# Two plain tile pairs per FFN, a weight queue that moves within a job, and a new order in the opening and the tail of a one-core decoder layer

## The chip, the core and the metric

One core of a Trainium2 chip runs the whole program. The metric is device time in microseconds (us) of one execution; a profiled execution gives the rows shown below. The engines are TensorE (PE in the rows, its weight loads PEld), VectorE (DVE), ScalarE (ACT), GpSimd (POOL, whose queue also issues some transfers) and SyncE (SP, which issues the others).

## What is computed

One decoder layer for a prompt of 1024 rows and for 8 single-row samples that share its weights, in float32:

```python
def pre(i, t):
    return rms_norm(t, norm_g[i]) * (1 + mod[:, :, 3 * i + 1]) + mod[:, :, 3 * i]   # mod = adaLN(c)
x = x + 0.5 * mod[:, :, 2] * swiglu(pre(0, x), ffn1_up, ffn1_down)
y, states = token_mix(pre(1, x), caches, ...)       # dilated attention + gMLP
x = x + mod[:, :, 5] * y
x = x + 0.5 * mod[:, :, 8] * swiglu(pre(2, x), ffn2_up, ffn2_down)
# after the layer: rms_norm(x, final_g); outputs also hold the key/value caches, one row further
def swiglu(h, w_up, w_down):
    a, b = jnp.split(h @ w_up, 2, axis=-1)
    return (jax.nn.silu(a) * b) @ w_down
```

The model width is 1024, the FFN width 2816 (22 tiles of 128), two FFNs and a token mix between them.

## The kernel before

The activations are held transposed, features on the partitions, 1032 columns (1024 prompt rows and 8 samples) as two halves of 516, each of two quarters of 258. Every float32 operand is split into a leading part (`hi`, a cast by ACT) and a remainder (`lo`, a subtraction by DVE), and each product is three matmuls: hi by hi, hi by lo, lo by hi.

**Up projection** (`Up`). For each of the 22 tiles the two blocks `a` and `b` of the weight are multiplied with the input. A *plain* tile pair goes through eight steps per half of the columns, each step 12 matmuls (four slices of the contraction by three) of 258 columns. A *factored* tile uses seven products in place of eight, each of two blocks of 12 matmuls, one per half. Its weights need sums of weight blocks (`take`, lines 701 to 705, DVE) and its activations need combinations of their quarters (`blend`, DVE and ACT). The first `PLAINS = 3` tiles are plain, in the order of `turns` (tile, half): (0,0), (1,0), (0,1), (1,1), (2,0), (2,1). Meanwhile the operands of the second half and the combinations are made by generators in `hi_q`, which `tick` moves on; there are two ticks in each block of 12 matmuls. `blend` for the second half waits with its last two operands for the end of the plain turns of each half (`plain_done`), since their buffers come from there. A tile's weight units are prepared six units ahead at most, and as buffers come free. `banks` gives the first PSUM bank of each plain turn; gates (lines 764 to 768) read a bank before the next turn may write it. After the combinations the adaLN stream of the later modulations starts in FFN 1.

**Down projection** (`Down`). The 22 tiles are five parts of 6, 4, 4, 4 and 4. Parts 1 to 4 in the order of the program (here called part 0 to part 3) run as eight whole-tile jobs each (`whole`, `mm_thirds`): 1032 columns in three pieces of 344, K slices by three pieces by three matmuls, so 54 in a job of part 0 and 36 in a job of parts 1 to 3. Line 321 is the matmul that needs the remainder of the weights. After a job DVE reads the sample columns (line 950) and adds the product to the residual in six pieces (line 954). The last part runs in narrower jobs.

The weights of the down projection come through a queue. SP loads a slab into one of two raw buffers; `advance` casts an operation's piece of it (line 249, ACT) and puts its subtraction `low_part` (line 252, DVE) on the list `late`, two ticks off; `pump` calls `advance` if the slab was issued at least two counts of `clock` ago and fewer than four operations are under way. `run` calls a job, counts the clock up, calls `pump` and gives one tick. A job that needs an operation whose subtraction is still on the list makes `get_wt` put it into the queue at once. A slab is given back, and the next load issued, when its last subtraction is queued. In part 0 an operation serves one job, in parts 1 to 3 two.

```python
if i not in raws or clock[0] - born[i] < 2 or st["op"] - st["done"] >= 4:
    return                                  # pump
...
while st["low"] <= i:                       # get_wt
    late.popleft()[1]()
```

The split of the next part's operands (`Down.split`, lines 872 and 874) is a generator of `hi_q` too; in part 0 it starts at the seventh tick.

**Opening.** Row statistics (`row_scale`: line 465 on DVE, 468 on ACT, 474 on POOL), scaling (`over_rms`) and transposes (`turned_x`) of four row tiles make the first half of the columns; the samples go through `smp`; the first four adaLN groups (`first_mods`, line 394, and `ada_fin`, lines 416 to 431) give shift and scale for `modulate` and `sample_norm`. Four steps of the first plain turn (`up1.step`) are placed by hand between them.

**Tail.** `finish_last` turns the last quarter back, scales rows by 1/rms and stores them; `scaled` (line 1887) is DVE, line 1924 ACT. Line 1876 applies `final_g` to the first 512 features of that quarter ahead of time.

Of the kernel before, what the change touches and what calls it, by code (L numbers as in the profile page):

```python
# [11 lines left out]
AF = mybir.ActivationFunctionType  # L12
# [53 lines left out]
def trunk(ctx: ExitStack, tc, a, o):  # L66
    nc = tc.nc
# [37 lines left out]
    def ends(t, n=4):  # L105

        return t.rearrange("p k (q t) -> p k q t", q=2)[:, :, :, 256:]
# [8 lines left out]
    def dealing(**kw):  # L116
        for k, v in kw.items():
            deal[k] = deque(v)
# [30 lines left out]
    clock = [0]  # L149
# [34 lines left out]
    for g in range(3):  # L184
        n = (LS[g] - 1) * 512
        for b in range(NS):
            s = a[f"cache_kv_g{g}"][0, b, 1:].rearrange("r k h d -> (r k h d)")
            t = o[6 + g][0, b, :LS[g] - 1].rearrange("r k h d -> (r k h d)")
# [3 lines left out]
            t = t.rearrange("(r c) -> r c", r=rows)  # L192
# [71 lines left out]
    def pump():  # L264
        if st["op"] >= st["last"]:
            return
        i, s = ops[st["op"]]
        if i not in raws or clock[0] - born[i] < 2 or st["op"] - st["done"] >= 4:
            return
        advance()  # L270
# [39 lines left out]
    def mm_thirds(w, j, K, act):  # L310

        ps = bank("three")[:, :, :CW]
        wt = get_wt(w)
        for k in range(K):
            wh, wl = wt.at(k, j)
            h, l = act(k)
            for c in range(3):
                cs = slice(c * CW, (c + 1) * CW)
                mm_f(ps[:, c], wh, h[:, cs], start=(k == 0), stop=False)  # L319
                mm_f(ps[:, c], wh, l[:, cs], start=False, stop=False)  # L320
                mm_f(ps[:, c], wl, h[:, cs], start=False, stop=(k == K - 1))  # L321
            if k < K - 1:
                tick()
                if k % 2:
                    tick()
        return ps
# [334 lines left out]
    class Up:  # L661

        ACC = (0, 1, 0, 2, 0, 2, 1)
        AHEAD = 6
        PLAINS = 3

        STEPS = ((0, 0, 0), (1, 0, 1), (0, None, 2), (1, None, 3), (2, 1, 0), (3, 1, 1), (2, 6, 2), (3, 6, 3))

        def __init__(self, w, dst):
            self.w = w[0].rearrange("(k p) c -> p k c", p=128)  # L670
            self.dst = dst
            self.turns = [(n, (p,)) for n, p in ((0, 0), (1, 0), (0, 1), (1, 1), (2, 0), (2, 1))]
            self.turns += [(n, (0, 1)) for n in range(self.PLAINS, NF)]
            self.units = [(n, j) for n in range(NF) for j in range(4 if n < self.PLAINS else 7)]
            self.base = {n: self.units.index((n, 0)) for n in range(NF)}
            self.left = [4 if n < self.PLAINS else 1 for n, j in self.units]
            self.n, self.next, self.top, self.gone = len(self.units), 0, 0, [0, 0]
            self.raw, self.wt, self.tmp = {}, {}, {}
# [302 lines left out]
    up1, down1 = Up(a["ffn1_up"], g_d), Down(a["ffn1_down"], g_d, xs_d, 16, XS)  # L981
# [26 lines left out]
    up2, down2 = Up(a["ffn2_up"], g_d), Down(a["ffn2_down"], g_d, x2_d, 64, None)  # L1008
# [45 lines left out]
    def turned_x(t, h, qs, ks=range(4)):  # L1054

        for k in ks:
            f = h * 4 + k
            nc.tensor.transpose(qs[k][:, t % 4 * 128:(t % 4 + 1) * 128], XN[t // 2][:, t % 2, f * 128:(f + 1) * 128], ident)
# [19 lines left out]
    def sample_norm(h):  # L1078
        v = SXT[0][:, 4 * h:4 * h + 4]
        nc.vector.tensor_tensor(v, v, MOD[:, 8 + 4 * h:12 + 4 * h, 1:9], op=ALU.mult)  # L1080
        for p in range(2):
            c = 4 * p
            nc.vector.tensor_tensor(ends(XT[p][h]), v[:, :, c:c + 4].rearrange("p k (q t) -> p k q t", q=2),
                                    MOD[:, 4 * h:4 * h + 4, 1 + c:5 + c].rearrange("p k (q t) -> p k q t", q=2), op=ALU.add)
# [9 lines left out]
    def steps(g, n=99):  # L1094
        for _ in range(n):
            if next(g, 0) == 0:
                return
# [3 lines left out]
    fins = {g: ada_fin(g) for g in range(4)}  # L1101
    XT[0], XT[1] = ([four(qb(name="x")) for h in range(2)] for p in range(2))
    smp = sample_rows()
# [7 lines left out]
    steps(mods[2])  # L1111
    steps(fins[2], 1)
    row_scale(1)
    steps(smp)
    got = [bank("nx") for k in range(4)]
    over_rms(0, 0)
    turned_x(0, 0, got)
    steps(fins[2])
    row_scale(2)
    over_rms(1, 0)  # L1120
    turned_x(1, 0, got)
    sample_norm(0)
    row_scale(3)
    for t in (2, 3):
# [13 lines left out]
    up1.step(0, 0, 0)  # L1138
    up1.prepare(2)
    up1.step(0, 1, 0)  # L1140
    steps(mods[3])
    got = [PSB[:, i, :] for i in (4, 6, 5, 7)]
    for t in range(4):
        turned_x(t, 1, got, (0,))
    steps(fins[1])
    steps(fins[3], 1)
    for t in range(4):
        turned_x(t, 1, got, (1,))
    up1.step(0, 2, 0)
    up1.prepare(3)  # L1150
    steps(fins[3])
    up1.step(0, 3, 0)
    sample_norm(1)
    for t in range(4):
        turned_x(t, 1, got, (2, 3))
    for k in range(4):
        modulate(0, 4 + k, got[k])
    steps(halves(0, 1, 1, 2))
    dealing(nx=(4, 5, 6, 7))

    def second_half():
        yield
# [36 lines left out]
        if n >= 8 and j == 2:  # L1199
            pump_copy()  # L1200

    up1.run(hook1, (2, 2, 4, 2, 6, 4), 4)

    def last1(m, p, qs):
        stat_pair(XT[p][m // 4][:, m % 4], m, p)
# [648 lines left out]
    fgc = R0[:, :8]  # L1854
# [6 lines left out]
        if n >= 4 and j == 2:  # L1861
            pump_copy()

    up2.run(hook2, (2, 4, 6, 2, 6, 4))

    SPOT = {(0, 0): (1024, 1540), (1, 0): (1540, 1798), (1, 1): (1024, 1282)}

    def last2(m, p, qs):
        key = p, qs[0]
        last = key == (1, 1)  # L1870
        c0, c1 = qs[0] * QW, (qs[-1] + 1) * QW
        x = XT[p][m // 4][:, m % 4, c0:c1]
        stat_add(x, m, key, ph[:, slice(*SPOT[key])], last and m == 7)
        if last and m < 4:
            v = x[:, :256]
            nc.scalar.activation(v, v, AF.Copy, scale=fgc[:, m:m + 1])
        if m == 7:
            hi_q.append(finish_last() if last else finish(p, qs))

# [5 lines left out]
    def scaled(row, w, hf, q, r):  # L1885
        f4 = lambda v: v.rearrange("p (f c) -> p f c", f=4)
        nc.vector.scalar_tensor_tensor(f4(row[:w, hf * 512:(hf + 1) * 512]), f4(q[:w, :]), r,
                                       f4(fgb[:w, hf * 512:(hf + 1) * 512]), op0=ALU.mult, op1=ALU.mult)
# [21 lines left out]
    def finish_last():  # L1910

        blks = [v for v in BLOCKS if v[0] // QW == 1]
        banks = {(n, hf): PSB[:, n * 2 + hf, :] for n in range(3) for hf in range(2)}
        for n, (b, w) in enumerate(blks[:2]):
            turned(1, b, w, 0, banks[n, 0])
        rs = yield from rstd((1, 1), shifted(blks, 1), 0, 0)
        for n, (b, w) in enumerate(blks[:2]):
            turned(1, b, w, 1, banks[n, 1])
        b2, w2 = blks[2]
        for hf in range(2):  # L1920
            turned(1, b2, w2, hf, banks[2, hf])
        rows_ = [rows2(qb(name="y"))[:, 0, :1024] for _ in blks]
        for n, (b, w) in enumerate(blks[:2]):
            nc.scalar.activation(rows_[n][:, :512], banks[n, 0], AF.Copy, scale=rs[n])
            scaled(rows_[n], w, 1, banks[n, 1], rs[n])
            nc.sync.dma_start(out_rows(1, b, w), rows_[n])
        for hf in range(2):
            scaled(rows_[2], w2, hf, banks[2, hf], rs[2])
        nc.sync.dma_start(out_rows(1, b2, w2), rows_[2][:w2])

    down2.run(last2, [(0, (0, 1)), (1, (0,)), (1, (1,))])
# [31 lines left out]
```

## Time and profile before

| | |
|---|---|
| median of 3 runs | 2442.7 us (2440.42 to 2444.96) |
| profiled execution | 2440.93 us |
| its span, first to last instruction | 2438.9 us |
| mean granted clock of TensorE | 0.986 of full speed |

A row of the timeline begins with the start in us from the begin of the span and the duration in us, then engine, line, operation, result and operands, and in brackets how long that engine was idle before and what ended the wait. A wait row names who waited for whom, the total in us, the number of waits and the longest. A window row gives a stretch, the busy us (and number) of engines in it, then the granted clock, the busy share of the DMA engines and GB/s. The ends of matmuls are modelled and neighbouring matmuls overlap, so rates are taken from start to start.

### The profile page before, as it was taken

The numbers are of one execution on the slowest core, as the hardware profiler recorded it, in microseconds if no ns is written. First come the engines' busy times: TensorE is split into PE (matmuls) and PEld (weight loads), VectorE is DVE, ScalarE is ACT, GpSimd is POOL, SyncE is SP. The second block draws the span as 40 slices with busy tenths as digits, with TensorE's granted clock in tenths as the row PEclk, the third lists the DMA queues.
The fourth block names the chain that finished last, engine by engine and source line by source line (L and its number), as shares of the span: only waits on it lengthen the run. The fifth ranks groups of instructions, "written<-read, shape, count | busy, mean of one in ns | idle before, by whom it ended". The sixth has DMA issues, their size and how long they took to land.

```text
span 2438.9 us, 42426 instructions
## 1 busy us (share of the span) xinstructions
PE 2363.5 (97%) x18047; PEld 2272.3 (93%) x18047; DVE 1278.2 (52%) x2674; ACT 759.6 (31%) x1455; POOL 251.6 (10%) x378
## 2 busy tenths in 40 slices
PE   7999999998899999999999999999999999988999
PEld 5999999997899999999998999999999999987998
DVE  5555555563466544333252534536566666644665
ACT  4433333341111344444421131224333333411112
POOL 1200000020000200001110012221000000100003
PEclk8999999999999999999999999999999999999999
DMA  8554565454310221123221127534455552443201
GB/s 290 106 181 153 172 190 182 157 212 152 122 70 29 88 78 46 62 77 107 86 76 57 40 84 227 175 106 126 152 194 185 183 183 79 137 159 122 70 18 70
DMA packets 203670, 305.00 MB, mean 125 GB/s; under 512 B 9081, under 2 KB 146017, under 8 KB 199898
## 3 DMA queue, kind: packets, MB, share of 16 engines
q1 hardware_dynamic: 177840, 206.38, 25.8%
q0 software_dynamic: 25488, 95.83, 12.1%
q8 instruction: 141, 2.31, 0.4%
q14 instruction: 47, 0.39, 0.1%
q10 hardware_dynamic: 154, 0.09, 0.0%
HBM read 245.72 MB, written 100.53 MB: 142 GB/s over the span
## 4 chain that ended last, share of the span: by engine, by line
PE 56%; issue 3%; DVE 3%; DMA 1%; ACT 1%; POOL 1%; DVEq 0%; POOLq 0%; ACTq 0%
PE PSB L287 6%; PE PSB L740 6%; PE PSB L741 6%; PE PSB L742 6%; PE PSB L288 5%; PE PSB L289 5%; PE PSB L303 3%; PE PSB L304 3%; PE PSB L305 3%; PE PSB L321 3%; PE PSB L320 3%; PE PSB L319 3%; PE PSB L1342 1%; PE PSB L1394 1%; PE PSB L1377 1%
## 5 line engine op out<-in xcount | busy, mean ns | idle before, releaser
L740 PE MATMUL PSB<-h,lo 128*128 128x258 f32 x1264 | 361.2, 286 | 2.8 <-DVE t L765 1.5
L287 PE MATMUL PSB<-n,hi 128*128 128x258 f32 (+1 forms) x1152 | 361.7, 314 | 1.8 <-DVE s L930 1.8
L741 PE MATMUL PSB<-h,lo 128*128 128x258 f32 x1264 | 358.1, 283 | 0.3 <-DVE h L573 0.3
L742 PE MATMUL PSB<-h,lo 128*128 128x258 f32 x1264 | 357.2, 283 | 0.0
L740 PE MATMUL PSB<-h,hi 128*128 128x258 f32 x1248 | 355.9, 285 | 1.2 <-DVE t L768 1.2
L741 PE MATMUL PSB<-h,hi 128*128 128x258 f32 x1248 | 353.2, 283 | 0.0
L742 PE MATMUL PSB<-h,hi 128*128 128x258 f32 x1248 | 352.2, 282 | 0.0
L288 PE MATMUL PSB<-n,hi 128*128 128x258 f32 (+1 forms) x1152 | 349.1, 303 | 0.5 <-DVE n L546 0.5
L289 PE MATMUL PSB<-n,lo 128*128 128x258 f32 (+1 forms) x1152 | 347.4, 302 | 0.0
L321 PE MATMUL PSB<-g,lo 128*128 128x344 f32 x864 | 285.6, 331 | 41.0 <-DVE lo L252 41.0
L319 PE MATMUL PSB<-g,hi 128*128 128x344 f32 x864 | 283.8, 328 | 2.2 <-DVE t L804 1.9
L320 PE MATMUL PSB<-g,hi 128*128 128x344 f32 x864 | 284.1, 329 | 0.0
L740 PEld LDWEIGHTS PSB<-h,lo 128*128 128x128 f32 x1264 | 239.9, 190 | 16.6 <-issue 10.1
L740 PEld LDWEIGHTS PSB<-h,hi 128*128 128x128 f32 x1248 | 236.4, 189 | 13.2 <-issue 10.6
L741 PEld LDWEIGHTS PSB<-h,lo 128*128 128x128 f32 x1264 | 240.0, 190 | 0.5 <-DVE h L573 0.5
L742 PEld LDWEIGHTS PSB<-h,lo 128*128 128x128 f32 x1264 | 239.5, 189 | 0.0
L287 PEld LDWEIGHTS PSB<-n,hi 128*128 128x128 f32 x1152 | 218.2, 189 | 22.5 <-issue 17.0
L741 PEld LDWEIGHTS PSB<-h,hi 128*128 128x128 f32 x1248 | 236.7, 190 | 0.0
L742 PEld LDWEIGHTS PSB<-h,hi 128*128 128x128 f32 x1248 | 236.0, 189 | 0.0
L249 ACT ACTIVATE hi<-raw 128x1024 fp32r<-128x1024 f32 (+1 forms) x114 | 114.0, 1006 | 358.2 <-PE PSB L320 212.8
L288 PEld LDWEIGHTS PSB<-n,hi 128*128 128x128 f32 x1152 | 218.4, 190 | 1.9 <-DVE n L546 1.7
L289 PEld LDWEIGHTS PSB<-n,lo 128*128 128x128 f32 x1152 | 218.4, 190 | 0.0
(299 smaller groups left out, 4426.9 us busy)
## 6 DMA issues: line engine op xcount, KB each, us to landing
raw<-in_ffn_up_dram SPq DMA_DIRECT2D x88, 512.0 KB, 5.6
ada<-in_ada_w_dram SPq DMA_DIRECT2D x36, 1024.0 KB, 6.0
out_dram<-in_cache_kv_g_dram SPq DMA_DIRECT2D x16, 2047.0 KB, 10.9
g<-g_d POOLq DMA_DIRECT2D x22, 1032.0 KB, 5.8
g_d<-t POOLq DMA_DIRECT2D x76, 258.0 KB, 2.7
raw<-in_ffn_down_dram SPq DMA_DIRECT2D x16, 1024.0 KB, 5.0
raw<-in_w_in_dram SPq DMA_DIRECT2D x12, 1024.0 KB, 5.2
raw<-in_w_in_dram SPq DMA_DIRECT2D x18, 512.0 KB, 3.7
```

Source lines behind the costliest of these rows:

```text
L249: nc.scalar.activation(h3, v, AF.Copy)
L287: mm_f(ps, wh, ah, start=(k == 0), stop=False)
L288: mm_f(ps, wh, al, start=False, stop=False)
L289: mm_f(ps, wl, ah, start=False, stop=(k == K - 1))
L303: mm_f(ps[:, q, :], wh, h, start=(k == 0), stop=False)
L304: mm_f(ps[:, q, :], wh, l, start=False, stop=False)
L319: mm_f(ps[:, c], wh, h[:, cs], start=(k == 0), stop=False)
L320: mm_f(ps[:, c], wh, l[:, cs], start=False, stop=False)
L321: mm_f(ps[:, c], wl, h[:, cs], start=False, stop=(k == K - 1))
L740: mm_f(out, wh, ah, start=(kk == 0 and start), stop=False, **go)
L741: mm_f(out, wh, al, start=False, stop=False, **go)
L742: mm_f(out, wl, ah, start=False, stop=(kk == 3 and stop), **go)
```

## The change

`PLAINS` goes from 3 to 2: the third tile becomes a factored one in both FFNs, the turns (2,0) and (2,1) go, and the bank lists of both up projections get four entries. In `mm_thirds` the clock counts up and `pump` is called once more, after the middle slice of the contraction. In the opening the statistics, scaling and transposes of the second row tile come ahead of the third adaLN group's end and of the samples; the ends of the second and fourth group and all transposes for two feature tiles come ahead of the third hand-placed step. In the tail the samples' rows of the last block are scaled by `final_g` early, together with the prompt rows, and their first half is scaled by ACT in place of DVE.

```diff
--- before.py
+++ after.py
@@ -319,6 +319,9 @@
                 mm_f(ps[:, c], wh, h[:, cs], start=(k == 0), stop=False)
                 mm_f(ps[:, c], wh, l[:, cs], start=False, stop=False)
                 mm_f(ps[:, c], wl, h[:, cs], start=False, stop=(k == K - 1))
+            if k == K // 2 - 1:
+                clock[0] += 1
+                pump()
             if k < K - 1:
                 tick()
                 if k % 2:
@@ -662,14 +665,14 @@
 
         ACC = (0, 1, 0, 2, 0, 2, 1)
         AHEAD = 6
-        PLAINS = 3
+        PLAINS = 2
 
         STEPS = ((0, 0, 0), (1, 0, 1), (0, None, 2), (1, None, 3), (2, 1, 0), (3, 1, 1), (2, 6, 2), (3, 6, 3))
 
         def __init__(self, w, dst):
             self.w = w[0].rearrange("(k p) c -> p k c", p=128)
             self.dst = dst
-            self.turns = [(n, (p,)) for n, p in ((0, 0), (1, 0), (0, 1), (1, 1), (2, 0), (2, 1))]
+            self.turns = [(n, (p,)) for n, p in ((0, 0), (1, 0), (0, 1), (1, 1))]
             self.turns += [(n, (0, 1)) for n in range(self.PLAINS, NF)]
             self.units = [(n, j) for n in range(NF) for j in range(4 if n < self.PLAINS else 7)]
             self.base = {n: self.units.index((n, 0)) for n in range(NF)}
@@ -1111,14 +1114,14 @@
     steps(mods[2])
     steps(fins[2], 1)
     row_scale(1)
-    steps(smp)
     got = [bank("nx") for k in range(4)]
     over_rms(0, 0)
     turned_x(0, 0, got)
-    steps(fins[2])
     row_scale(2)
     over_rms(1, 0)
     turned_x(1, 0, got)
+    steps(fins[2])
+    steps(smp)
     sample_norm(0)
     row_scale(3)
     for t in (2, 3):
@@ -1138,25 +1141,23 @@
     up1.step(0, 0, 0)
     up1.prepare(2)
     up1.step(0, 1, 0)
+    steps(fins[1])
     steps(mods[3])
+    steps(fins[3], 1)
     got = [PSB[:, i, :] for i in (4, 6, 5, 7)]
     for t in range(4):
-        turned_x(t, 1, got, (0,))
-    steps(fins[1])
-    steps(fins[3], 1)
-    for t in range(4):
-        turned_x(t, 1, got, (1,))
+        turned_x(t, 1, got, (0, 1))
+    steps(fins[3])
+    sample_norm(1)
     up1.step(0, 2, 0)
     up1.prepare(3)
-    steps(fins[3])
-    up1.step(0, 3, 0)
-    sample_norm(1)
     for t in range(4):
         turned_x(t, 1, got, (2, 3))
+    up1.step(0, 3, 0)
     for k in range(4):
         modulate(0, 4 + k, got[k])
     steps(halves(0, 1, 1, 2))
-    dealing(nx=(4, 5, 6, 7))
+    dealing(nx=(4, 5, 6, 7), tr=(6, 7))
 
     def second_half():
         yield
@@ -1199,7 +1200,7 @@
         if n >= 8 and j == 2:
             pump_copy()
 
-    up1.run(hook1, (2, 2, 4, 2, 6, 4), 4)
+    up1.run(hook1, (2, 2, 4, 6), 4)
 
     def last1(m, p, qs):
         stat_pair(XT[p][m // 4][:, m % 4], m, p)
@@ -1861,7 +1862,7 @@
         if n >= 4 and j == 2:
             pump_copy()
 
-    up2.run(hook2, (2, 4, 6, 2, 6, 4))
+    up2.run(hook2, (2, 4, 6, 4))
 
     SPOT = {(0, 0): (1024, 1540), (1, 0): (1540, 1798), (1, 1): (1024, 1282)}
 
@@ -1872,8 +1873,7 @@
         x = XT[p][m // 4][:, m % 4, c0:c1]
         stat_add(x, m, key, ph[:, slice(*SPOT[key])], last and m == 7)
         if last and m < 4:
-            v = x[:, :256]
-            nc.scalar.activation(v, v, AF.Copy, scale=fgc[:, m:m + 1])
+            nc.scalar.activation(x, x, AF.Copy, scale=fgc[:, m:m + 1])
         if m == 7:
             hi_q.append(finish_last() if last else finish(p, qs))
 
@@ -1924,8 +1924,8 @@
             nc.scalar.activation(rows_[n][:, :512], banks[n, 0], AF.Copy, scale=rs[n])
             scaled(rows_[n], w, 1, banks[n, 1], rs[n])
             nc.sync.dma_start(out_rows(1, b, w), rows_[n])
-        for hf in range(2):
-            scaled(rows_[2], w2, hf, banks[2, hf], rs[2])
+        nc.scalar.activation(rows_[2][:w2, :512], banks[2, 0][:w2], AF.Copy, scale=rs[2])
+        scaled(rows_[2], w2, 1, banks[2, 1], rs[2])
         nc.sync.dma_start(out_rows(1, b2, w2), rows_[2][:w2])
 
     down2.run(last2, [(0, (0, 1)), (1, (0,)), (1, (1,))])
```

## Rows read from the trace of the kernel before

**Rows 1.** The page: busy time of each engine; granted clock in 40 equal slices.

```profile
PE 2363.5 (97%) x18047; PEld 2272.3 (93%) x18047; DVE 1278.2 (52%) x2674; ACT 759.6 (31%) x1455; POOL 251.6 (10%) x378
...
PEclk8999999999999999999999999999999999999999
```

**Rows 2.** The list of waits of TensorE: us in total, times, longest.

```profile
PE PSB L321 <- DVE lo L252: 41.0, 14, 3.2
```

**Rows 3.** Windows, TensorE alone: stretch, its us, busy (matmuls), clock, DMA share, GB/s.

```profile
554.00:569.10 15.10, 15.10 (x96) 1.00 0.83 304
...
569.10:582.80 13.70, 10.13 (x54) 0.88 0.40 147
...
582.80:594.40 11.60, 8.77 (x57) 1.00 0.21 68
...
645.90:656.50 10.60, 7.50 (x39) 0.84 0.42 153
...
700.00:750.00 50.00, 50.00 (x319) 1.00 0.18 64
```

**Rows 4.** The timeline of DVE and PE at one job's end, part 0, FFN 1.

```profile
593.97 0.16 DVE L950 TENSOR_TENSOR s<-PSB,MOD 128x2 f32<-128x2 f32 x1 [7.60 <-PE PSB L321]
...
595.06 1.90 DVE L954 SCALAR_TENSOR_TENSOR x<-PSB,MOD,x 128x256 f32<-128x256 f32 x6
...
597.02 0.95 DVE L252 TENSOR_TENSOR lo<-raw,hi 128x768 fp32r<-128x768 f32 x1
...
598.02 0.42 PE L321 MATMUL PSB<-g,lo 128*128 128x344 f32 x1 [2.83 <-DVE lo L252]
```

**Rows 5.** The timeline of DVE: first banks of jobs, FFN 1 and 2.

```profile
559.67 0.16 DVE L950 TENSOR_TENSOR s<-PSB,MOD 128x2 f32<-128x2 f32 x1 [5.23 <-PE PSB L321]
...
655.58 0.16 DVE L950 TENSOR_TENSOR s<-PSB,MOD 128x2 f32<-128x2 f32 x1 [4.02 <-PE PSB L321]
...
666.96 0.16 DVE L950 TENSOR_TENSOR s<-PSB,MOD 128x2 f32<-128x2 f32 x1 [1.42 <-PE PSB L321]
...
2146.69 0.16 DVE L950 TENSOR_TENSOR s<-PSB,MOD 128x2 f32<-128x2 f32 x1 [4.39 <-PE PSB L321]
...
2242.26 0.16 DVE L950 TENSOR_TENSOR s<-PSB,MOD 128x2 f32<-128x2 f32 x1 [4.01 <-PE PSB L321]
```

**Rows 6.** The timeline of ACT in part 0, FFN 1.

```profile
563.72 2.03 ACT L872 ACTIVATE g<-g 128x1032 fp32r<-128x1032 f32 x2 [10.74 <-DMA g<-g_d]
...
568.56 3.03 ACT L249 ACTIVATE hi<-raw 128x768 fp32r<-128x768 f32 x4
...
590.84 0.85 ACT L249 ACTIVATE hi<-raw 128x768 fp32r<-128x768 f32 x1 [19.25 <-DMA raw<-in_ffn_down_dram]
```

**Rows 7.** Windows: busy us (number) of PE, PEld, DVE, ACT, POOL; clock, DMA, GB/s.

```profile
1800.00:1900.00 100.00, 100.00 (x836) 100.00 (x835) 62.43 (x95) 36.19 (x65) 6.99 (x10) 1.00 0.53 185
```

**Rows 8.** The timeline of DVE and ACT around the plain turns, both FFNs.

```profile
101.94 0.42 DVE L765 SCALAR_TENSOR_TENSOR t<-t,PSB 128x258 f32<-128x258 f32 x1
...
104.67 0.69 DVE L701 TENSOR_TENSOR raw<-raw 128x512 f32<-128x512 f32 x1
...
110.09 0.39 ACT L764 ACTIVATE t<-PSB 128x258 f32<-128x258 f32 x1 [3.34 <-PE PSB L742]
...
1729.48 0.42 DVE L765 SCALAR_TENSOR_TENSOR t<-t,PSB 128x258 f32<-128x258 f32 x1 [5.22 <-ACT t L764]
```

**Rows 9.** The timeline of the opening.

```profile
18.84 1.95 PE L1074 MATMUL PSB<-t,cs 8*128 8x8 f32 x16 [0.72 <-ACT t L416]
...
36.33 0.16 PEld L394 LDWEIGHTS PSB<-ada,ph 128*32 128x32 f32 x8 [1.48 <-DMA ada<-in_ada_w_dram]
...
44.32 0.39 PE L740 MATMUL PSB<-h,lo 128*128 128x258 f32 x1 [1.28 <-ACT h L572]
```

**Rows 10.** The timeline of the tail.

```profile
2432.82 1.26 ACT L1924 ACTIVATE y<-PSB,s 128x512 f32<-128x512 f32 x2 [2.07 <-POOL s L508]
...
2432.82 2.71 DVE L1887 SCALAR_TENSOR_TENSOR y<-PSB,s,ph 128x512 f32<-128x512 f32 x4 [0.77 <-POOL s L508]
```

## Prediction

> **What bounds the kernel now.** I read the page first: the matrix engine is busy for 97% of the span, in nearly every slice of it, and the granted clock stands a little lower in the first slice alone [rows 1]. So the path that sets the end is the engine's own stream of matmuls, and a change can gain in three ways only: fewer matmuls, shorter waits of that engine, or less time at its lower clock. The second view is the list of what it waits for. One entry holds more than half of all its idle time: the third matmul of a weight block (line 321, which uses the remainder part of the weights) waits for the vector engine's subtraction on line 252, 41.0 us in 14 waits [rows 2]. Line 321 stands in whole-tile jobs alone, so this is the down projection. The windows then say what these waits cost besides themselves. Just before them the stretch is full and at clock 1.00. From 569 us on it is not: two of the three windows shown with waits have 0.84 to 0.88, a mixture of the 2.4 and the 1.2 GHz level, and one has 1.00 although it holds a wait as well. Jobs of the same kind without waits run at 1.00 again [rows 3].
>
> The timeline of one job shows where a wait comes from [rows 4]. The job's first bank is read at 593.97, the six pieces of the residual go from 595.06 to 596.96, and only then comes the subtraction for the next job's weights, at 597.02. The matrix engine, idle for 2.83 us, goes on at 598.02. So the cast of the weights was not late, only their remainder: it was put into the vector engine's queue at the moment the job began that needs it, behind the evacuation of the job before.
>
> **The change part by part.** *The pump in mid-job.* I stepped through `pump`, `advance`, `low_part` and `tick` by hand, job by job. Today `pump` is called once per job, after the evacuation; the remainder is due two ticks later, the job's end gives one, and the next job asks for it at once, so it is forced. In the first part (eight weight blocks, one per job) this meets blocks 2 to 8: seven forced remainders per FFN, fourteen in all, just the count of the waits. In parts 1 to 3 a block serves two jobs and nothing is forced. With the change the clock moves twice per job, so block 2 is taken one call earlier (after job 0), and blocks 3 and 5 in the middle of jobs 1 and 2. Six ticks or more then lie before use; every remainder is queued at least one whole job ahead. From then on the limit of four blocks under way stops further mid-job calls, and from part 1's sixth job on the sequence is that of today.
>
> Price: from the first bank of job 0 to the first bank of part 1's job 0 lie 6 + 7 x 54 + 30 = 414 matmuls. The pace without waits is two jobs of 36 in 666.96 - 655.58 = 11.38 us, 0.1581 us each. That makes 65.4 us; the trace took 95.9 in the first FFN and 95.6 in the second [rows 5]. What is lost is 30.5 + 30.1 = 60.6 us: 41.0 of waits and 19.6 at the lower clock. I take all of it, because nothing takes the wait's place. The casts on the scalar engine do move: block 2's now stands behind the first of four operand splits for part 1 and not behind all four. That split starts at 563.72 when its transfer lands, takes about a microsecond, and job 2 begins at about 569.1 (60 matmuls after 559.67), so cast (0.8) and subtraction (0.95) have some 2 us to spare [rows 4 to 6]. Today the four casts at 568.56 run in one go, so buffers and the first two loads are there; the next is held only by a load that was issued late, at 590.84 [rows 6]. That load follows the remainder of block 3, which is now over ten microseconds earlier. If the first split came 4 us later, one wait of some 3 us would stay. Bounds: 52 to 61 us gained.
>
> *The third tile pair.* A plain pair takes 2 x 8 steps, a factored one 7 products x 2, each of 12 matmuls: 24 fewer in each FFN. The steady stretch has 836 in 100 us, 0.12 us each, so 2.9 us per FFN [rows 7]. What is added is work of other engines at the changeover: the combinations of the second half's operands and the sums of weight blocks are due a turn and a half earlier. In the second FFN the vector engine stands idle 5.22 us just there, which hides the four weight sums of 0.69 us (2.8 us): the whole 2.9 us is gained [rows 8]. In the first FFN it is different. Its gate on bank 0 is at 101.94, done at 102.36; the next turn starts at about 102.9 (its fifth step ends at 110.09, and five steps are 7.2 us). There is 0.5 us to spare, and the four weight sums, which today start at 104.67, come before that gate [rows 8]. So bank 0 is late by about 2.0 us, and bank 1, behind one more combination, by a little more: I take 2.6 us off. Net gain 0.3 us, between -2 (with a stretch at the lower clock behind it) and 2.9. The adaLN stream starts a turn and a half sooner, and one cache copy moves from the first FFN to the second; both are transfers with room in a DMA share near 0.5, at nothing. If that room were gone, a late weight block would cost a wait like the longest of today, 3.2 us [rows 2].
>
> *The opening.* The last adaLN group lands, after a wait of 1.48 us, at 36.33, and the first step that needs it starts at 44.32 [rows 9]. Between them today stands a plain step of 12 matmuls (1.4 us) in front of the transposes of that group; it now comes behind them, and one transpose group comes before the second step. That takes 1.4 us out of the chain. Against it: the samples' 16 small matmuls, 1.95 us, now lie ahead of the fourth row statistic, which I make 0.6 us later; the wait before 36.33 hides most of that. I take 1.2 us, between -1 and 2.5. The `tr` entry repeats the banks that it had.
>
> *The tail.* The vector engine ends with four scalings in 2.71 us, one after the other, and the program's last store waits for them [rows 10]. One of the four goes to the scalar engine, whose own two take 1.26 us from the same start: 0.65 us, between 0 and 0.7. The two more columns scaled on line 1876 cost nothing, hidden under the row of matmuls.
>
> Sum: 60.6 + 2.9 + 0.3 + 1.2 + 0.65 = 65.7 us. The profiled execution took 2440.93 us (span 2438.9), so 2375.3; the median of the runs is 1.8 us above it, so **2377 us**.
>
> **The rivals.** *Waits come back at the loads.* The remainder is queued early, but its cast waits for a transfer, as the one at 590.84 does today. If three of seven jobs in each FFN kept their loss, 26 us would stay: 2403. Against it: the loads are released by the earlier remainders themselves, and a stretch with weights, operands and residual together moved 304 GB/s [rows 3].
>
> *The lower clock is not the waits' doing.* Then 41.0 us go and 19.6 stay: 2397. For it: a wait of the same kind at 582.8 to 594.4 left the clock at 1.00. Against it: every stretch without waits has 1.00 [rows 3]. Beside this stands the Trainium skill, "TensorE: Matmul & The Clock Gate", section "Why this matters for your kernels": it warns of idle gaps between bursts of matmuls that are longer than these; by it such waits should cost only themselves, and the sum would be 46 us. The trace disagrees with it in these windows.
>
> *The mid-job call does nothing,* because its conditions (load old enough, fewer than four blocks ahead) fail each time. Then only the small parts remain, about 5 us: 2437.5, no more than a measurement can tell.
>
> *Slower than before:* with its pauses gone, the engine is granted the lower clock under dense work in the first part of each down projection. At 1.2 GHz throughout, 2 x 8 jobs of 54 x 0.158 us, 137 us, would take twice as long: 2514. It decides against the change when the mean clock there is under about 0.66. Against it: 100% busy stretches at 1.00 in parts 1 to 3 and in the up projection [rows 3, 7].
>
> **How the numbers follow.** Forecast as worked out 0.78, with its own range 2371 to 2384; waits at the loads 0.07; clock stays low 0.05; an Up changeover that costs ten microseconds or more 0.03 (2390); nothing in mid-job 0.04; slower 0.03. About 0.2%, 5 us, is what a measurement of this kernel can tell from no change. So faster 0.93, same 0.04, slower 0.03. The range, 2370 to 2389, takes in the bounds of the changeover, the opening and one kept wait per FFN; it leaves out the load, no-effect and slower cases.
>
> **What would show it.** Right: the entry of line 321 against line 252 gone or under 5 us; the stretch between the two first-bank reads near 65.4 us in both FFNs at clock 1.00; subtractions of line 252 in front of the six residual pieces, not behind; 24 fewer matmuls on lines 740 to 742 in each FFN; a new wait of 2 to 3 us against lines 765 or 768 near 103 us, none near 1733; the step at 44.32 about a microsecond earlier; three scalings at the end. Wrong: line 319 or 320 waiting for a cast or a transfer in the first part, a clock under 1.00 there without a wait, or waits of line 740 for operand combinations after the changeover.

## The result and the profile after

| | before | after |
|---|---|---|
| median | 2441.96 us (4 runs, 2440.42 to 2444.96) | 2376.87 us (4 runs, 2376.49 to 2379.57) |
| profiled execution | 2440.93 us | 2377.03 us |
| its span | 2438.9 us | 2375.2 us |
| mean granted clock | 0.986 | 0.993 |

The ratio is 0.9734, with a 95% interval of 0.9718 to 0.9751: 65 us less, where 65.7 were forecast. The page of after (busy time of each engine, granted clock in 40 slices) answers to [rows 1]:

```profile
PE 2337.8 (98%) x17999; PEld 2253.4 (95%) x17999; DVE 1291.1 (54%) x2687; ACT 768.8 (32%) x1466; POOL 250.6 (11%) x374
...
PEclk8999999999999999999999999999999999999999
```

There are 48 matmuls fewer, 24 in each FFN. In the list of TensorE's waits the entry of [rows 2] is gone. What is new, or longer than it was, are waits at the gates (lines 768 and 771 of after are 765 and 768 of before) and one in the opening (line 1061):

```profile
PE PSB L743 <- DVE t L768: 4.2, 2, 2.7
PE PSB L1061 <- ACT xn L1053: 2.9, 1, 2.9
PE PSB L743 <- DVE t L771: 2.8, 4, 1.2
```

The timeline of after, of DVE and in one row of PE. The rows of line 953 at 558.18, 634.83, 2113.02 and 2189.80 are the first banks that answer to [rows 5] (the second and the fourth are those of part 1's third job). Between them stand a remainder that comes early, the end of one job of part 0, to be laid beside [rows 4], and the first matmul of that part's last job:

```profile
558.18 0.16 DVE L953 TENSOR_TENSOR s<-PSB,MOD 128x2 f32<-128x2 f32 x1 [3.69 <-PE PSB L321]
...
564.50 0.95 DVE L252 TENSOR_TENSOR lo<-raw,hi 128x768 fp32r<-128x768 f32 x1
...
583.76 0.16 DVE L953 TENSOR_TENSOR s<-PSB,MOD 128x2 f32<-128x2 f32 x1 [4.52 <-PE PSB L321]
...
584.85 1.90 DVE L957 SCALAR_TENSOR_TENSOR x<-PSB,MOD,x 128x256 f32<-128x256 f32 x6
...
586.81 0.95 DVE L252 TENSOR_TENSOR lo<-raw,hi 128x768 fp32r<-128x768 f32 x1
...
610.09 0.31 PE L319 MATMUL PSB<-g,hi 128*128 128x344 f32 x1
...
634.83 0.16 DVE L953 TENSOR_TENSOR s<-PSB,MOD 128x2 f32<-128x2 f32 x1 [1.38 <-PE PSB L321]
...
2113.02 0.16 DVE L953 TENSOR_TENSOR s<-PSB,MOD 128x2 f32<-128x2 f32 x1 [4.40 <-PE PSB L321]
...
2189.80 0.16 DVE L953 TENSOR_TENSOR s<-PSB,MOD 128x2 f32<-128x2 f32 x1 [1.38 <-PE PSB L321]
```

From the first bank of job 0 to that of part 1's third job the forecast is 65.4 + 11.38 = 76.8 us; the trace has 76.65 and 76.78. At 586.81 the subtraction still stands behind the six residual pieces, just as before, and not in front of them, as the forecast's sign had it. But it now serves the part's last job, which begins 23 us later, at 610.09, and nothing waits for it. The remainder with the least time to spare is that of block 2: it is done at 565.45, and its job begins at 567.45, so the 2 us to spare of the forecast are there. Windows over the same work, TensorE alone (stretch, us, busy and matmuls, clock, DMA share, GB/s), against [rows 3]:

```profile
569.00:583.00 14.00, 14.00 (x91) 1.00 0.74 273
583.00:594.00 11.00, 11.00 (x72) 1.00 0.29 95
620.00:632.00 12.00, 12.00 (x79) 1.00 0.63 214
```

By stages the span's 63.7 us come off like this: 1.5 before the first down projection's first bank (559.67 to 558.18), 30.6 from there to part 1's third job (107.29 to 76.65), 1.5 from there to the second down projection's first bank (1479.73 to 1478.19), 30.0 behind it. The two whole-tile stretches alone make 60.8 of it (30.6, and in the second FFN 106.91 to 76.78). All else gave 2.9, where 5.05 were forecast.

### The profile page after: what moved, and what is told of

It reads as the page before. It is cut to its first block, busy times and chain, and to the rows that moved or that the text cites. A ratio compares the mean times of both kernels' runs of the same rounds, so it can differ in the third digit from the quotient of the medians.

```text
span 2375.2 us, 42343 instructions
## 1 busy us (share of the span) xinstructions
PE 2337.8 (98%) x17999; PEld 2253.4 (95%) x17999; DVE 1291.1 (54%) x2687; ACT 768.8 (32%) x1466; POOL 250.6 (11%) x374
## 4 chain that ended last, share of the span: by engine, by line
PE 62%; DVE 2%; ACT 1%; issue 0%; DVEq 0%; POOL 0%; ACTq 0%
PE PSB L287 7%; PE PSB L288 6%; PE PSB L289 6%; PE PSB L743 6%; PE PSB L744 6%; PE PSB L745 6%; PE PSB L303 3%; PE PSB L304 3%; PE PSB L305 3%; PE PSB L320 3%; PE PSB L321 3%; PE PSB L319 3%; PE PSB L1343 1%; PE PSB L1395 1%; PE PSB L1378 1%; PE PSB L1592 1%
## 5 line engine op out<-in xcount | busy, mean ns | idle before, releaser
L743 PE MATMUL PSB<-h,lo 128*128 128x258 f32 x1248 | 356.9, 286 | 4.6 <-DVE t L768 4.2
L744 PE MATMUL PSB<-h,lo 128*128 128x258 f32 x1248 | 353.2, 283 | 0.3 <-DVE h L576 0.3
L745 PE MATMUL PSB<-h,lo 128*128 128x258 f32 x1248 | 352.3, 282 | 0.0
L320 PE MATMUL PSB<-g,hi 128*128 128x344 f32 x864 | 276.6, 320 | 0.0
L321 PE MATMUL PSB<-g,lo 128*128 128x344 f32 x864 | 276.4, 320 | 0.0
L319 PE MATMUL PSB<-g,hi 128*128 128x344 f32 x864 | 275.8, 319 | 0.0
L743 PEld LDWEIGHTS PSB<-h,lo 128*128 128x128 f32 x1248 | 236.4, 189 | 18.4 <-issue 10.1
L744 PEld LDWEIGHTS PSB<-h,lo 128*128 128x128 f32 x1248 | 236.7, 190 | 0.5 <-DVE h L576 0.5
L745 PEld LDWEIGHTS PSB<-h,lo 128*128 128x128 f32 x1248 | 236.1, 189 | 0.0
```

The costliest lines, as they stand in the source:

```text
L743: mm_f(out, wh, ah, start=(kk == 0 and start), stop=False, **go)
L744: mm_f(out, wh, al, start=False, stop=False, **go)
L745: mm_f(out, wl, ah, start=False, stop=(kk == 3 and stop), **go)
```

## The experiments

The ratios are to the kernel before on the same chip, each with its interval; us are the ratio times the median of before there (2443.9 to 2446.9). The first four kernels each take one part of the change alone.

**e1: the call in the middle alone.** The edit is the diff's first hunk on the kernel before.

> The kernel before with the call in the middle of whole-tile jobs alone. Theory (the prediction's): the call costs nothing, all 14 waits of the matrix engine on the remainder go (41.0 us), and with them the stretches at the lower clock that followed them (19.6 us): 60.6 us less than before, 52 to 61. Rival 1: the lower clock is a matter of the work, not of the waits: about 41 us less. Rival 2, from the trace of the changed kernel (its first banks stand 30.6 and 30.1 us closer in the two projections): 60.8 us less, and the granted clock in the first down projection 1.00.

Measured: 0.9744 (0.9731 to 0.9758), 62.6 us less (59.2 to 65.8). The entry of line 321 is gone. The forecast of 60.6 and the trace's 60.8 are both inside; 41 is not. So the lower clock in these stretches was the waits' doing: with them it goes.

**e2: two plain pairs alone.** The edit is `PLAINS = 2`, the four `turns` and the two bank lists.

> The kernel before with two plain tile pairs per FFN in place of three, alone. Theory A (the prediction's): 2.9 us less in the second FFN, 0.3 us less in the first (2.9 of matmuls against a wait of 2.6 at the changeover): 3.2 us less in all. Theory B (from the trace of the changed kernel): in the second FFN about 1.5 us less; in the first nothing of its own, since the down projection's start waits there for an operand split that hangs on a transfer: the end of the up projection can move by about 2 us and only that wait changes. 1.5 us less in all, between 0.5 and 3.

Measured: 0.9969 (0.9957 to 0.9981), 7.6 us less (4.6 to 10.5). Both theories are too small. In the second FFN its trace has what was forecast: from the first wait of the up projection (1699.80, before 1698.15) to the down projection's first matmul (2137.66, before 2138.91) 2.9 us less. In the first FFN the changeover waits as forecast (3.1 us), and still the stage as a whole gains. The list of waits of before has an entry of line 319, the down projection's first matmul:

```profile
PE PSB L319 <- DVE t L804: 1.9, 1, 1.9
```

Line 804 is an addition of the up projection's last tile. It stands in DVE's queue right behind the subtraction of the operand split, and so it is late when the split is late. This wait is 0.2 in e2, and from that matmul to the first bank it takes 7.8 us, not 9.4. Where that comes from is the subject of e9 to e12.

**e3 and e4: the opening alone, the tail alone.** The edits are the hunks at lines 1111 to 1160, and those at 1872 and 1924.

> The kernel before with the new order of the opening alone (row statistics ahead of the samples). Theory A (the prediction's): 1.2 us less. Theory B (from the trace of the changed kernel, where the fourth step begins 0.35 us later, not earlier): the up projection starts 0.35 us later; that is either hidden by the down projection's start (no change in the time) or shown (0.4 us more).

> The kernel before with the new end alone (one scaling of the samples' last store by the scalar engine, the last tile's scale over the whole of it). Theory A (the prediction's): 0.65 us less, the length of one scaling on the vector engine. Theory B (from the trace of the changed kernel, where the store of 128 rows now lands last): 0.07 us less, which no measurement tells from no change.

Measured: e3 0.9994 (0.9985 to 1.0003), e4 0.9995 (0.9986 to 1.0004). Neither is to be told from no change, so their theories can't be told apart by the time either; the traces are read below.

**e5 and e6: place or lead, and the price of one wait.** e5 leaves the call where it was and takes younger loads; e6 has the call in the middle, but without the count.

```diff
-        if i not in raws or clock[0] - born[i] < 2 or st["op"] - st["done"] >= 4:
+        if i not in raws or clock[0] - born[i] < 1 or st["op"] - st["done"] >= 4:
```

> The kernel before with one number changed: a block of weights may be taken one job after its load was issued, not two. No call in the middle of a job. Theory A: the waits went because the remainder now stands a whole job ahead of its use, not because of the place in the middle; by the queue's rules no remainder is then left to its own job, so 60 to 62 us less, as with the call in the middle alone. Theory B: the place in the middle is needed, because after the job's end the cast and the remainder come behind the residual's pieces; then most of the 41 us of waits stays and the gain is under 20 us. Rival C: the younger load has not landed one job (8.5 us) after its issue; the cast then waits for it and the matrix engine behind it, some us for each of up to 8 loads per FFN, and the gain is 20 to 50 us.

```diff
             if k == K // 2 - 1:
-                clock[0] += 1
                 pump()
```

> The kernel before with the call in the middle of whole-tile jobs, but without counting the half job in the age of a load. By the queue's rules one block per FFN (that of the third job) still gets its remainder within its own job, so two waits of 2.8 to 3.2 us in all stay, in place of none. Theory A (each wait costs its length and on average 19.6 / 14 = 1.4 us of lower clock): 8 to 9 us of the 62 come back, 53 to 54 us less than before. Theory B (the lower clock needs several waits in a row, one alone costs its length): 6 us come back, 56 us less.

Measured: e5 0.9747 (0.9734 to 0.976), 61.9 us less, the same as e1. So the call in the middle is not needed: it is enough that the queue runs one job ahead. e6: 0.9779 (0.9766 to 0.9793), 54.1 us less. The call without the count already takes 12 of the 14 waits away, so either of the two, younger loads or more calls, does all or most of it. Two waits are left, and some 8 us come back, as theory A has it; the intervals leave 6 open. The trace of e6 tells more, since it has the two waits at the same job of the two FFNs. First the matmuls that waited (timeline of PE), then the windows around them:

```profile
574.39 0.66 PE L321 MATMUL PSB<-g,lo 128*128 128x344 f32 x1 [3.23 <-DVE lo L252]
...
2134.45 0.43 PE L321 MATMUL PSB<-g,lo 128*128 128x344 f32 x1 [2.83 <-DVE lo L252]
```

```profile
574.40:580.00 5.60, 5.60 (x19) 0.50 0.71 244
580.00:590.00 10.00, 10.00 (x63) 0.98 0.00 0
...
2134.40:2140.00 5.60, 5.55 (x35) 1.00 0.59 185
```

Behind the first wait 5.6 us pass at the 1.2 GHz level, 19 matmuls where 35 fit behind the second. The one wait costs 2.5 us (16 matmuls of 0.158) besides itself, the other nothing at the clock. The kernel before shows the same on waits of one length. The matmul at 586.42 had waited 2.83 us, as had the one at 598.02 [rows 4]; its row, and then the windows of 5.5 us from the one and from the other:

```profile
586.42 0.42 PE L321 MATMUL PSB<-g,lo 128*128 128x344 f32 x1 [2.83 <-DVE lo L252]
```

```profile
586.42:591.92 5.50, 5.50 (x35) 1.00 0.44 143
598.02:603.52 5.50, 5.50 (x25) 0.69 0.00 0
```

Of its 14 waits ten are followed by a window like the second, with 25 matmuls, and four by one like the first; the length of the wait does not decide it. The Trainium skill, "TensorE: Matmul & The Clock Gate", section "Why this matters for your kernels", warns only of idle gaps longer than those of 2.83 us; the row of 598.02 disagrees.

**e7 and e8: the opening undone, the changeover mended.** e7 is the changed kernel with the old opening. In e8 the weight sums are kept from the vector engine until the last plain turn's gates are through:

```diff
-            self.prepare(min(self.top + self.AHEAD, self.gone[-2] + 7))
+            end = min(self.top + self.AHEAD, self.gone[-2] + 7)
+            self.prepare(min(end, self.base[self.PLAINS] + 1) if hold else end)
...
-                    self.ahead(i, self.STEPS[j][0])
+                    self.ahead(i, self.STEPS[j][0], (i, p) < (self.PLAINS - 1, 1) or j < 6)
```

> The changed kernel with the opening's old order put back. Theory A (the prediction's): 1.2 us more than the changed kernel, 2378.1. Theory B (from the opening alone, where the fourth step began no earlier than in two other runs of the old order): no difference, 2377, within 1 us.

> The changed kernel, and in the plain turns the weight blocks from the first factored tile's third one on (those whose sums occupy the vector engine) are not prepared before the last plain turn's step 6. Theory A: the wait at the changeover (3.1 us) goes, and all of it shows: 2373.8. Theory B: the wait goes, but the down projection's start is then held by its operand split, which ended just in time in the changed kernel: 0 to 1.5 us of it show, 2375.4 to 2376.9. Theory C: the sums only move, and the first factored products wait for their weights in place of the gate: 2377 or more, with a wait of 1 to 3 us on a weight tile after the changeover.

Measured: e7 2376.21 us, 0.9715 (0.9702 to 0.9728); e8 2378.64 us, 0.9724 (0.971 to 0.9737). Both intervals overlap that of the changed kernel, so the time alone doesn't decide between the theories of e7; its trace comes back below. By its ratio e7 is 69.7 us less than before (66.6 to 72.9), as much as e1 and e2 together (62.6 + 7.6 = 70.2), so these two parts add up. In e8 the two changeover waits are gone, and 1.7 us of waiting for the evacuation on ACT (line 793) stands in their place: theory C, with another engine than it named.

**e9 to e12: the cache copy beside the down projection's start.** With one turn fewer, the first up projection issues 16 cache copies and not 17. The copy in its last turn is then another one, of half the size. The lists of transfers issued around that turn (operation, number, KB each), first in before and then in after:

```profile
out_dram<-in_cache_kv_g_dram SPq DMA_DIRECT2D x1, 2047.0 KB
```

```profile
out_dram<-in_cache_kv_g_dram SPq DMA_DIRECT2D x1, 1022.0 KB
```

Right behind it the load is issued on which the down projection's last first-part operands hang. e10 makes the copy small in the kernel before, e11 makes it large in the changed one, e12 has none in that turn, and e9 is the changed kernel beside them.

```diff
e10 (on before)        -        if n >= 8 and j == 2:
                       +        if n >= 9 and j == 2:
e11 (on after)         +        if n >= 7 and j == 2:
e12 (on after)         +        if 7 <= n < len(up1.turns) - 1 and j == 2:
```

> The changed kernel itself once more, beside the three below on one chip. All theories: a ratio of 0.972 to 0.975 to the kernel before. It is what the other three are compared with, and what the runs without the new opening (0.9715) and with the held sums (0.9724) are compared with.

> The kernel before, with the cache copies of the first up projection begun one turn later: 16 copies in place of 17, so that the copy beside the last turn is the last one of 1 MB in place of the first one of 2 MB, as it is in the kernels with two plain pairs. Theory A: this copy is what delays the load of 1 MB on which the down projection's first operands hang (10.3 to 12.2 us from issue to landing with three plain pairs, 8.3 to 8.9 with two); the load takes 8 to 9 us, the wait of 1.9 to 3.7 at the down projection's start goes to under 1, and 2 to 4 us less are to be seen, some 1.5 of it from the stretch at the lower clock behind that wait. Theory B: the load is quicker with two pairs for another reason (an earlier issue, other traffic): still 10 to 12 us, and no difference in time.

> The changed kernel, with the cache copies begun one turn earlier: 17 copies, so that the copy beside the last turn is the first one of 2 MB again. Theory A: the load takes 10 to 12 us from issue to landing, a wait of 1.5 to 3.5 us stands at the down projection's start, and the time is 2 to 4 us over that of the changed kernel. Theory B: no wait, no difference.

> The changed kernel, with 16 copies as it has, but one turn earlier each, so that none is issued in the last turn. Theory A: the load takes 6 to 8 us (its median over the whole kernel is 5.8), the start of the down projection has no wait in any run, and the time is that of the changed kernel or up to 1 us less. Theory B: the copies of the turn before are still moving, and nothing changes.

Measured: e9 2378.58 us, 0.9731 (0.9718 to 0.9744). e10 0.9987 (0.9979 to 0.9996), 3.2 us less than before (1.0 to 5.1). e11 2384.43 us, 5.9 more than e9; its runs (2382.47 to 2385.45) and those of e9 (2377.77 to 2379.82) don't meet. e12 2377.16 us, not to be told from e9. The rows of e9 and then of e11: the load's issue (POOL), the split that needs it (ACT), the down projection's first matmul (PE). For e11 there are also the split's subtraction and the addition behind it on DVE, which that matmul waits for, and the window behind the matmul.

```profile
540.69 0.55 POOL L865 DMA_DIRECT2D g<-g_d  x1 [3.62 <-PE PSB L745]
...
549.16 2.02 ACT L875 ACTIVATE g<-g 128x1032 fp32r<-128x1032 f32 x2 [0.84 <-DMA g<-g_d]
...
553.38 0.39 PE L319 MATMUL PSB<-g,hi 128*128 128x344 f32 x1
```

```profile
540.35 0.55 POOL L865 DMA_DIRECT2D g<-g_d  x1 [3.62 <-PE PSB L745]
...
551.98 2.02 ACT L875 ACTIVATE g<-g 128x1032 fp32r<-128x1032 f32 x2 [4.00 <-DMA g<-g_d]
...
553.08 2.38 DVE L877 TENSOR_TENSOR g<-g,g 128x1032 fp32r<-128x1032 f32 x2 [4.38 <-ACT g L875]
555.37 0.68 DVE L807 TENSOR_TENSOR t<-t,PSB 128x516 f32<-128x516 f32 x1
...
556.20 0.47 PE L319 MATMUL PSB<-g,hi 128*128 128x344 f32 x1 [3.20 <-DVE t L807]
```

```profile
556.00:560.00 4.00, 3.80 (x14) 0.57 1.04 355
```

From the load's issue to the split it is 8.5 us with the small copy and 11.6 with the large one; 10.3 in the trace of before, 8.3 in that of after; 7.6 and 7.5 in e10 and e12, where the split no longer waits for it. With the large copy line 319 then waits 3.2 us, and the stretch behind it has a clock of 0.57. In all fourteen traces, the wait of line 319 was 1.9 to 3.7 us in the seven with the large copy, and 0.9 or less in the seven with the small one or none. From the first matmul to the first bank it took 9.3 to 9.4 us in six of the former (the other one 7.8) and 7.8 to 7.9 in all of the latter. In e12, with no copy there, the load lands 6.1 us after its issue.

No version beat the changed kernel by more than the measurements can tell; e7 has the lowest ratio.

## Why the prediction was right, point by point

**The pump in mid-job** was right in its mechanism and its size: 60.6 us forecast, 62.6 measured alone, 60.8 by the first banks, at clock 1.00. e5 and e6 add what the text didn't say: of the two things that the change does there, the earlier age of the load is enough, and the extra call alone does most of it. One split of the sum was not quite right: it put all of the 19.6 us beside the waits down to the lower clock. The windows behind the waits show some 16 (ten times 10 matmuls of 0.158). The rest goes with every wait, at the full clock too. From the first bank of before at 582.37 to the one at 593.97 [rows 4] it is 11.60 us, with the wait of 2.83 that ends at 586.42 and the full clock between them; 54 matmuls (8.53) and the wait alone would make 11.36:

```profile
582.37 0.16 DVE L950 TENSOR_TENSOR s<-PSB,MOD 128x2 f32<-128x2 f32 x1 [9.16 <-PE PSB L321]
```

All of it is gone with the waits. The rival of the lower clock fell with e1. That of waits at the loads fell with the trace: in the first part no entry of line 319 or 320 waits for a cast there. The slower rival fell too, since the full stretches keep 1.00 (its bound for the mean clock, 0.66, is 0.68 by its own numbers, 137 over 137 + 65.7; nothing hung on it).

**The third tile pair.** The 2.9 us of the second FFN: 2.9 in e2's trace, 1.3 in that of after, from the first wait to the down projection (1665.77 to 2105.24 against 1698.15 to 2138.91). A new wait at 1691.56 takes 0.4 in both. The rest is a matter of the steady stretch, which the forecast took as fixed [rows 7]. The timeline of ACT, the same evacuation in two tiles that are 14 apart, first in e2 and then in after:

```profile
1804.89 0.60 ACT L795 ACTIVATE t<-PSB 128x516 f32<-128x516 f32 x1 [0.95 <-PE PSB L742]
...
2086.20 0.60 ACT L795 ACTIVATE t<-PSB 128x516 f32<-128x516 f32 x1 [0.95 <-PE PSB L742]
```

```profile
1771.13 0.60 ACT L798 ACTIVATE t<-PSB 128x516 f32<-128x516 f32 x1 [0.95 <-PE PSB L745]
...
2053.55 0.60 ACT L798 ACTIVATE t<-PSB 128x516 f32<-128x516 f32 x1 [0.96 <-PE PSB L745]
```

That is 281.31 us against 282.42, and 281.96 in before, with TensorE busy throughout at clock 1.00. It goes with the kernel, not with the execution (after and e9, the same kernel twice, have the same 20.17): a tile takes 20.09 us in both kernels with two pairs and the old opening (e2, e7), 20.17 in all five with two pairs and the new one, 20.13 to 20.14 in all seven with three pairs. Over some 19 tiles the 0.08 makes 1.5 of the 1.6 us that after lacks beside e2. That e2 has the full 2.9 in spite of the new wait is partly luck: its tiles are faster than those of before by 0.05. So the opening's new order, together with two pairs, costs 1.5 us in the second FFN. By which way (other buffers in the rings would be one) no run showed.

The first FFN's changeover was forecast with 2.6 us of waiting. The trace of after has 3.1, behind the weight sums as described; the gate of line 768, its late one, is at 106.28:

```profile
106.75 0.39 PE L743 MATMUL PSB<-h,lo 128*128 128x258 f32 x1 [2.72 <-DVE t L768]
...
108.83 0.39 PE L743 MATMUL PSB<-h,lo 128*128 128x258 f32 x1 [0.36 <-DVE t L771]
```

The step that failed is the sentence "one cache copy moves from the first FFN to the second; both are transfers with room in a DMA share near 0.5, at nothing". It priced the copy by the mean of the stage. Where the copy goes out, the last turn before the down projection, operands, residual and weights are loaded at once, and the DMA share is 1.02. A window of before:

```profile
536.00:550.00 14.00, 12.35 (x104) 1.00 1.02 377
```

There the missing megabyte is worth 3.2 us (e10) to 5.9 us (e11). That is as much as the tile itself. It is also why e2 gained more than either theory had. The forecast was also silent on the wait of 1.9 us at line 319, which was in the list of waits of before and is what this pays.

**The opening** was forecast with 1.2 us less, and the sign is not borne out. The second matmul of the fifth step (line 741 of before) starts at 44.56 to 46.20 in eight traces with the old order, 45.3 in the mean, and at 44.72 to 46.90 in six with the new one, 45.9 in the mean; the two overlap. The step that failed is the working's term for the samples: it took their 16 small matmuls at the old 1.95 us and the fourth row statistic at 0.6 us later. The timeline of after (PE and DVE) shows them at 3.58 us, the statistic behind their copy at 27.85, and TensorE waiting for its result:

```profile
23.57 3.58 PE L1077 MATMUL PSB<-t,cs 8*128 8x8 f32 x16
...
27.18 0.22 DVE L1079 COPY t<-PSB 128x64 f32<-128x64 f32 x1 [2.74 <-PE PSB L1077]
...
27.85 0.68 DVE L468 SCALAR_TENSOR_TENSOR t<-xin 128x512 f32<-128x512 f32 x1
...
30.19 1.11 PE L1061 MATMUL PSB<-cst,xn 128*128 128x128 f32 x4 [2.00 <-DVE xn L1055]
```

In before that statistic is at 24.57, so it is 3.3 us late and not 0.6. The small matmuls are slower because they now lie in a stretch in which the granted clock is at the 1.2 GHz level. The windows over them, of before and then of after:

```profile
18.84:20.79 1.95, 1.95 (x17) 1.00 1.06 343
```

```profile
23.57:27.15 3.58, 3.58 (x18) 0.50 1.05 385
```

All five other traces of the new order have the 3.58 us as well; the eight of the old order have 1.95 to 3.55. The wait of 1.28 us for the operand split at 44.32 [rows 9] did go. The wait of 2.9 us for `xn` of ACT in the list of after's waits is new. The waits for `xn` of DVE, of which the row of 30.19 is one, add up to the same in both kernels, in before and then in after:

```profile
PE PSB L1058 <- DVE xn L1052: 2.7, 2, 2.3
```

```profile
PE PSB L1061 <- DVE xn L1055: 2.7, 2, 2.0
```

With the slower tiles of the second FFN the new order loses some 2 us by these traces (an estimate, 0.6 and 1.5) where 1.2 were to be gained; the times can't tell it from nothing (e3, e7). e7, without it, has the lowest ratio of the kernels with the other parts, though not by more than the intervals allow.

**The tail** had the wrong path: 0.65 us forecast, 0.07 found. The timeline of SP in before, and then those of DVE, ACT and SP in after:

```profile
2433.64 0.99 SPq L1926 DMA_DIRECT2D out_dram<-y  x2
2435.57 0.26 SPq L1929 DMA_DIRECT2D out_dram<-y  x1
```

```profile
2369.19 2.05 DVE L1887 SCALAR_TENSOR_TENSOR y<-PSB,s,ph 128x512 f32<-128x512 f32 x3 [0.77 <-POOL s L511]
...
2370.00 0.99 SPq L1926 DMA_DIRECT2D out_dram<-y  x2
...
2370.34 0.66 ACT L1927 ACTIVATE y<-PSB,s 2x512 f32<-2x512 f32 x1
...
2371.30 0.28 SPq L1929 DMA_DIRECT2D out_dram<-y  x1
```

The scalings end 0.66 us sooner [rows 10] and the last store is issued 2.11 us after their start and not 2.75. But from that start to the end of the span it is 6.01 us, where it was 6.08. The step that failed is "the program's last store waits for them": it does, but the end didn't hang on when it was issued. The last to be issued is a store of two rows (8 KB). In both traces the larger store before it (512 KB) is issued 1.5 us after the start of the scalings, has landed 4.8 us after it, and the small one is complete 0.1 us behind that, though it was issued 0.6 us sooner in after. By these times of landing the larger store set the end in both kernels, and the change doesn't move it.

So the sum came out right because the 60.6 us carried it. Of the small parts two came to nothing or less (the opening and the tail), and one that was priced at nothing (the copy, 3 us or more) made up for much of that; that the whole lies within 1 us of the forecast is luck as far as these terms go.

## What to carry to other kernels

When an engine waits for a small piece of work that a queue hands out job by job, count the calls and ticks by hand before anything else: here one job of lead was worth 62 us, and a single constant gives it as well as a new call. Before a last instruction is made faster, look at which transfer the end really hangs on. Price a moved transfer by the DMA share of the stretch where it lands, not of the stage: whoever shortens a loop that also issues background transfers shifts which of them lies beside the next stage's start. And put the clock into the price of a wait, here between next to nothing and nearly its own length again, as a range.

## What the runs showed of the hardware

Waits of the same length were not followed by the same clock: of the 14 waits of the kernel before (2.83 to 3.23 us) ten cost some 1.6 us more at the clock (25 matmuls in place of 35 in the 5.5 us behind them) and four nothing; of e6's two the one 2.5 us, the other nothing. A load of 1032 KB, which lands in 5.8 us in the median over the kernel before, took 6.1 us with no copy issued in that turn (e12), 7.5 to 9.2 with a copy of 1 MB issued ahead of it on another queue, and 10.3 to 12.1 with one of 2 MB. And stretches of the same matmuls, dense and at clock 1.00, ran at different paces within 0.4% (20.09, 20.13, 20.14 and 20.17 us a tile), to the hundredth the same in every trace of kernels that agree in the opening and the number of plain pairs; the cause stays open. A store of two rows, issued 0.6 us sooner behind one of 128 rows, was complete no sooner.
